# Graph attention on one core: two of five index windows unpacked later, and four filler matmuls fewer, at the seam between the sort and the block loop

## The chip, the cores and the metric

The kernel runs on one core of a Trainium2 chip. A core has five engines that run their own instruction streams in order and meet through semaphores: TensorE (PE, matmul), VectorE (DVE), ScalarE (ACT), GpSimd (POOL) and SyncE (SP, which here only issues DMA transfers). The metric is the device time of one execution in microseconds (us). Lower is better.

## The reference, cut to what matters

The problem is one graph attention layer: 4096 nodes with 64 features, 50000 edges, 4 heads, 64 output features for each head.

```python
x_proj[h] = x @ weight[h]
src_att = np.sum(x_proj[h, src_nodes] * att_src[h], axis=-1)
dst_att = np.sum(x_proj[h, dst_nodes] * att_dst[h], axis=-1)
s = src_att + dst_att
s = np.where(s > 0, s, 0.2 * s)
# for every edge i:
output[h, dst[i]] += np.exp(s[h, i]) * x_proj[h, src[i]]
# for every node:
output[h, dst] /= (sum of np.exp(s[h, i]) over its edges + 1e-8)
```

The result has 4096 rows of 256 numbers (4 heads by 64).

## The kernel before, in words

**Stages.** The first 109 us or so sort the edges, in two rounds of a sorting network on DVE, into 16 groups of 256 source nodes each and, inside a group, by destination. After that the destinations are taken in 33 blocks (`ND`) of 125 nodes (`BD`). A block has 16 stretches of edges, one for each source group, and each stretch is a row of 128 slots (`W2`). An edge slot is a pair of small numbers: its destination within the block and its source within the group.

**The windows.** The sorted keys lie in DRAM. Five indirect gathers (L362, issued by POOL) bring 128 rows of 128 keys each into `win`. Window `i` of the five holds the rows of eight blocks, 8`i` to 8`i`+7. `Windows.unpack(i)` (L439 to L447) takes one window apart. Two DVE operations (L441, L442) cut the key into its two parts, two more operations (L445, L446) turn these into bf16 and subtract the block's offset, and one transfer on the SP queue (L447) writes 64 KB into the DRAM table `bin_dram` (`gat_bins` in the profile). For window 0, L445 and L446 run on DVE. For the other four windows they run on POOL.

**One block.** `Blocks.load(b)` (L466) reads row `b` of the table, 8 KB, and repeats it over all 128 partitions, 1 MB in all, into one of four `bc` buffers. `onehot(b)` (L483) compares it with the partition number on DVE (L493 and L495), which gives 0/1 matrices `oh`. `gather(b, c)` (L499), for three chunks `c` of 6, 6 and 4 source groups, multiplies them on PE with the node table `xa` and the destination table `adb` (L514, L516, L520). ACT then takes the exponentials `ex` (L522) and a copy `xs` (L524) from PSUM. `weights(b)` (L534, DVE) forms the edge weight `wv`, and `values(b)` (L542, DVE) the products `val`. `sums(b, k)` (L560 and L567, PE) adds up the edges of each destination in the PSUM tile `acc`. The sink's `take` copies `acc` out on ACT (L621, L623), `project` multiplies with the weights on PE (L629), `invert` and `give` (L634, L642, DVE) divide, and the SP queue writes the 125 rows out (L644).

**The order of the work** is written out by hand, under a manual schedule, so each engine runs its instructions in the order of the code. Step `b` of `Blocks.run` is: load of block b+4, values(b), the first gather of block b+1, project(b-1), sums(b,-1), the other two gathers of block b+1, invert(b-1), onehot(b+2) with weights(b+1) between its two halves, give(b-1), sums(b,0), sums(b,1). Blocks 0 and 1 are handled by hand before that loop, since the table is not in DRAM yet: `spread` (L472) repeats their rows with matmuls on PE (L479) and copies (L481) instead of a transfer.

**The fillers.** `busy(n)` (L711) issues n matmuls of 128x512 (L715) whose result nobody reads. They go into a PSUM tile with the tag of `acc`, of which there is one. They stand at three places: 9 in the sort, 11 after `longest`, and 3 ahead of the block loop.

The seam that the change touches reads, shortened:

```python
        busy(11)
        win.unpack(0)
        ...
            blocks.spread(1, c, win.tb[:, 0], lambda t: NT + t, S.copy if c < 2 else V.tensor_copy)
        ...
        for i in range(1, NI):
            win.unpack(i)
        blocks.sums(0, 1)
        busy(3)
        blocks.onehot(2)
        blocks.weights(1)
        blocks.run(1)
```

Of the kernel before, what the change touches and what calls it, by code (L numbers as in the profile page):

```python
# [38 lines left out]
def kernel(ctx: ExitStack, tc: tile.TileContext, x: bass.AP, edge_index: bass.AP,  # L39
# [8 lines left out]
    NI = -(-ND // 8)  # L48
# [288 lines left out]
    def longest(pool, pp, *sides):  # L337

        ps = pp.tile([1, len(sides), P], F32, name="mx_ps")
        for i, (ws, we) in enumerate(sides):  # L340
            mx = pool.tile([P, ws.shape[1]], F32, name=f"mx{i}")
            V.tensor_tensor(out=mx[:], in0=we[:], in1=ws[:], op=OP.subtract)
            mx1 = pool.tile([P, 1], F32, name=f"mxr{i}")
            V.tensor_reduce(out=mx1[:], in_=mx[:], axis=AX, op=OP.max)
            T.transpose(out=ps[:, i, :], in_=mx1[:], identity=ident[:])
        V.tensor_reduce(out=most[:, 2 - len(sides):2], in_=ps[:], axis=AX, op=OP.max)
# [18 lines left out]
    def group(pool, pp, start, between=(), busy=None):  # L365

        raw = pool.tile([P, L], F32, name="raw")
        fetch(pool, skey1, start, W1, raw, 1)
        kr = pool.tile([P, L], F32, name="kr")
        S.activation(out=kr[:], in_=raw[:], func=ACTF.Identity, bias=goff[:, 0:1])  # L370
        sgn = below(pool, kr[:], L, nb2, ND, 8 * NI)
        so = Sorter(pool, raw)
        so.rows(9)
        st = Stretches(pool, counts(pool, pp, sgn, 8 * NI, [sel2[:]])[0])
        if between:
            busy(9)
        ki = pool.tile([P, L], I32, name="ki")
        quiet = lambda keys: None
        store(skey2, so.runs(ki, FINE, [lambda keys: st.count(), *(between or (quiet, quiet)),
                                        *(lambda keys, f=f: f() for f in st.steps(0))]))  # L380
        return st
# [72 lines left out]
    class Blocks:  # L454
# [124 lines left out]
            self.onehot(1)  # L579
            self.weights(0)  # L580

        def run(self, first=0):
            for b in range(first, ND):
                self.load(b + 4)
                self.values(b, 2 if b == ND - 1 else 1)
                self.gather(b + 1, 0)
                if b:
                    self.sink.project(b - 1)
                self.sums(b, -1)
                self.gather(b + 1, 1)  # L590
                self.gather(b + 1, 2)

                if b:
                    self.sink.invert(b - 1)
                self.onehot(b + 2, halves=(0,))
                self.weights(b + 1)
                self.onehot(b + 2, halves=(1,))
                if b:
                    self.sink.give(b - 1)
                self.sums(b, 0)  # L600
                self.sums(b, 1)
            self.sink.project(ND - 1)
            self.sink.invert(ND - 1)
            self.sink.give(ND - 1, 2)
# [61 lines left out]
    def advance(pool, ws, we, w, what):  # L666

        n = ws.shape[1]
        at = pool.tile([P, n], F32, name=f"at{what}")
        gone = pool.tile([P, n], F32, name=f"gone{what}")  # L670
        V.tensor_tensor(out=gone[:], in0=ws[:], in1=we[:], op=OP.is_ge)
        V.tensor_scalar(out=at[:], in0=ws[:], scalar1=-1.0, scalar2=float(P * L), op0=OP.mult, op1=OP.add)
        V.tensor_tensor(out=at[:], in0=at[:], in1=gone[:], op=OP.mult)
        V.tensor_tensor(out=at[:], in0=at[:], in1=ws[:], op=OP.add)
        V.tensor_scalar(out=ws[:], in0=ws[:], scalar1=float(w), scalar2=None, op0=OP.add)
        return at
# [24 lines left out]
    with ExitStack() as st:  # L701
        so2 = st.enter_context(tc.tile_pool(name="sort2", bufs=1))
        blocks = Blocks(st, Finish(st))

        class Lent:


            def tile(self, shape, dt, name):
                return blocks.sink.psf.tile(shape, dt, name=name, tag="pf")

        def busy(n):  # L711

            t = blocks.psa.tile([P, L], F32, name="warm", tag="acc")
            for i in range(n):
                T.matmul(out=t[:], lhsT=identb[:], rhs=adb[:, 0:4, 0:P], start=True, stop=True)  # L715


        kb0 = so2.tile([P, W2], I32)
        t0 = so2.tile([P, 2, W2], I32)
        tb0 = so2.tile([P, 2, W2], BF16)  # L720

        def relative(keys):
            V.tensor_scalar(out=kb0[:], in0=keys[:, 0:W2], scalar1=goff[:, 0:1], scalar2=None, op0=OP.add)

        def split(keys):
            V.tensor_scalar(out=t0[:, 0, :], in0=kb0[:], scalar1=8, scalar2=None, op0=OP.logical_shift_right)
            V.tensor_scalar(out=t0[:, 1, :], in0=kb0[:], scalar1=SG - 1, scalar2=None, op0=OP.bitwise_and)
            S.copy(out=tb0[:], in_=t0[:])
            for c in range(len(CH)):
                blocks.spread(0, c, tb0[:], lambda t: RUN * t, S.copy)  # L730

        stretches = group(so2, Lent(), wi1[:], (relative, split), busy)
        win = Windows(cst, stretches.to[0][:])
        for c in range(len(CH)):
            blocks.onehot(0, *CH[c])
            blocks.gather(0, c)
        stretches.rest()
        longest(so2, Lent(), (ws1, we1), (ws2, we2))
        V.tensor_scalar(out=over[:], in0=most[:, 0:1], scalar1=float(W1), scalar2=None, op0=OP.is_gt)
        V.scalar_tensor_tensor(out=over[:], in0=most[:, 1:2], scalar=float(W2), in1=over[:], op0=OP.is_gt, op1=OP.max)  # L740
        busy(11)
        win.unpack(0)
        for b in range(2, 5):
            blocks.load(b)
        blocks.weights(0)
        blocks.values(0)
        for c in range(len(CH)):
            blocks.spread(1, c, win.tb[:, 0], lambda t: NT + t, S.copy if c < 2 else V.tensor_copy)
            if c == 1:
                blocks.onehot(1, *CH[0])  # L750
        for c in (1, 2):
            blocks.onehot(1, *CH[c])
        blocks.sums(0, -1)
        blocks.gather(1, 0)
        blocks.sums(0, 0)
        blocks.gather(1, 1)
        blocks.gather(1, 2)
        for i in range(1, NI):
            win.unpack(i)
        blocks.sums(0, 1)  # L760
        busy(3)
        blocks.onehot(2)
        blocks.weights(1)
        blocks.run(1)
        again = nc.values_load(over[0:1, 0:1], min_val=0, max_val=1, skip_runtime_bounds_check_because="0 or 1")
    order.close()

# [1 line left out]
    with tc.If(again > 0):  # L769
        n1 = room(0, EL)  # L770
        with tc.tile_pool(name="all", bufs=1) as al:
            total = al.tile([P, ND, AW], F32)
            V.memset(total[:], 0.0)
            with tc.For_i(0, n1, W1):
# [5 lines left out]
                with tc.For_i(0, m2, W2):  # L780
                    with ExitStack() as st:
                        win = Windows(st.enter_context(tc.tile_pool(name="win", bufs=1)), advance(al, ws2, we2, W2, 2)[:])
                        for i in range(NI):
                            win.unpack(i)
                        blocks = Blocks(st, Total(total))
# [42 lines left out]
```

## Time and profile before

| quantity | value |
|---|---|
| median of 14 runs | 290.75 us (288.94 to 292.1) |
| the profiled execution's own time | 291.22 us |
| its span, first to last instruction | 289.4 us |
| mean granted TensorE clock | 0.869 of full speed |
| busy: DVE, PE, ACT, POOL | 259.2, 204.7, 190.9, 34.1 us |
| the block loop, L542 of block 1 to the last result | about 131.8 to 283 us |

The profile gives times in microseconds from the span's start. A row of its timeline has the start, the duration, the engine, the line of the kernel, what the operation writes and reads, and, in square brackets, how long the engine stood idle before it and what ended that idle time. "PEld" is PE's loading of stationary operands, "SPq" an issue on the SP queue. Shares of busy time are averages over stages with different limits, so they don't tell which engine sets the end in one stage.

### The profile page before, as it was taken

To read this page: it belongs to the slowest core of one execution; us is meant where nothing else is said; L and a number is where in the kernel's file an instruction comes from. 1 tells how busy PE (TensorE), PEld (TensorE's weight loads), DVE (VectorE), ACT (ScalarE), POOL (GpSimd) and SP (SyncE) were. 2 spreads that over 40 slices of the span, in tenths; PEclk is the share of its full clock that TensorE was granted. 3 is DMA by queue.
4 is the path that set the end of the run, shared out by engine and by line. 5 is a ranking of instruction groups with operands and counts; after the bars stand their busy time and mean duration, and the time that the engine had idled before them with its cause. 6 is when DMAs were issued, how large, how long until landed. Compare 5 with 4: busy or idle time off the path is not lost.

```text
span 289.4 us, 8530 instructions
## 1 busy us (share of the span) xinstructions
PE 204.7 (71%) x3531; PEld 194.6 (67%) x3531; DVE 259.2 (90%) x526; ACT 190.9 (66%) x392; POOL 34.1 (12%) x81
## 2 busy tenths in 40 slices
PE   0011899970000055769999999999999999999990
PEld 0010599960000025558999999999999999999980
DVE  5999999993599999858999999999999999999970
ACT  2960720022599938554888888888888888888860
POOL 7882000001100001851000000000000000000000
PEclk9999975555555559997999999999999999999997
DMA  3016000000100001495676776767686868675011
GB/s 111 0 46 119 0 2 0 0 2 36 36 0 0 0 0 40 143 348 186 202 280 229 275 240 254 263 233 273 226 285 220 292 206 297 215 284 186 23 38 43
DMA packets 12688, 40.77 MB, mean 141 GB/s; under 512 B 1840, under 2 KB 8272, under 8 KB 8672
## 3 DMA queue, kind: packets, MB, share of 16 engines
q1 hardware_dynamic: 10128, 37.91, 36.9%
q10 hardware_dynamic: 1808, 1.56, 2.3%
q0 software_dynamic: 704, 0.66, 1.2%
q8 instruction: 30, 0.49, 0.7%
q14 instruction: 18, 0.15, 0.2%
HBM read 35.08 MB, written 5.05 MB: 139 GB/s over the span
## 4 chain that ended last, share of the span: by engine, by line


## 5 line engine op out<-in xcount | busy, mean ns | idle before, releaser
L524 ACT CAST xs<-ps 128x1200 bf16<-128x1200 f32 (+1 forms) x99 | 104.1, 1052 | 0.0
L542 DVE TENSOR_TENSOR val<-xs,wv 128x4096 bf16<-128x4096 bf16 (+1 forms) x34 | 75.4, 2219 | 0.4 <-ACT xs L524 0.2
L516 PE MATMUL ps<-adb,oh 128*128 128x136 bf16 x528 | 62.1, 224 | 0.0
L514 PE MATMUL ps<-xa,oh 128*128 128x72 bf16 x528 | 59.4, 197 | 3.7 <-DVE oh L493 2.1
L567 PE MATMUL acc<-xs,val 128*128 128x125 bf16 x1024 | 61.8, 218 | 0.0
L567 PEld LDWEIGHTS <-val 128*128 128x128 bf16 x1056 | 58.5, 98 | 0.3 <-DVE val L542 0.3
L516 PEld LDWEIGHTS <-oh 128*128 128x128 bf16 x528 | 49.5, 99 | 1.5 <-issue 1.3
L514 PEld LDWEIGHTS <-oh 128*128 128x128 bf16 x528 | 47.3, 99 | 3.2 <-DVE oh L493 3.2
L281 PE MATMUL cnt_ps<-sgn,sel 128*128 128x17 f32 (+1 forms) x6 | 1.6, 387 | 60.4 <-ACT sgn L273 41.1
L493 DVE TENSOR_SCALAR oh<-bc,pF 128x4096 bf16<-128x4096 bf16 (+2 forms) x37 | 42.5, 1148 | 0.8 <-ACT bc L481 0.8
L281 PEld LDWEIGHTS cnt_ps<-sgn,sel 128*128 128x128 f32 x6 | 1.4, 320 | 60.4 <-issue 60.4
L522 ACT ACTIVATE ex<-ps 128x96 bf16<-128x96 f32 (+1 forms) x99 | 25.0, 252 | 25.8 <-PE ps L520 25.7
L202 DVE TENSOR_TENSOR sA<-sB 128x256 f32<-128x256 f32 (+2 forms) x104 | 37.2, 399 | 1.5
L202 DVE TENSOR_TENSOR sB<-sA 128x256 f32<-128x256 f32 (+2 forms) x98 | 35.1, 399 | 1.3
L520 PE MATMUL ps<-xa,oh 128*128 128x72 bf16 x528 | 33.6, 198 | 0.1
L520 PEld LDWEIGHTS <-oh 128*128 128x128 bf16 x528 | 26.5, 99 | 0.2 <-DVE oh L495 0.2
L420 PEld LDWEIGHTS at_ps<-uv,xT 64*128 64x128 f32 x130 | 25.7, 307 | 0.2 <-issue 0.2
L420 PE MATMUL at_ps<-uv,xT 64*128 64x4 f32 x130 | 25.8, 335 | 0.0
L495 DVE TENSOR_SCALAR oh<-bc,pF 128x2048 bf16<-128x2048 bf16 (+2 forms) x37 | 25.6, 692 | 0.0
L270 ACT ACTIVATE junk<-kr,nb 128x512 f32<-128x512 f32 x33 | 23.8, 722 | 1.1
L629 PE MATMUL pf<-Wbd,aT 128*128 128x128 f32 (+1 forms) x132 | 23.3, 299 | 0.5 <-ACT aT L621 0.5
L560 PEld LDWEIGHTS <-xs 128*128 128x128 bf16 x528 | 18.7, 97 | 0.4
(141 smaller groups left out, 230.5 us busy)
## 6 DMA issues: line engine op xcount, KB each, us to landing
bc<-gat_bins SPq DMA_DIRECT2D x31, 1024.0 KB, 5.2
out_dram<-res SPq DMA_DIRECT2D x32, 125.0 KB
eD<-in_edge_index_dram ACTq DMA_DIRECT2D x2, 195.0 KB, 3.5
eS<-in_edge_index_dram SPq DMA_DIRECT2D x2, 195.0 KB
gat_bins<-tb SPq DMA_DIRECT2D x5, 64.0 KB, 5.2
gat_sorted<-sA SPq DMA_DIRECT2D x1, 256.0 KB, 2.0
gat_sorted<-ki SPq DMA_DIRECT2D x1, 256.0 KB
win<-gat_sorted,to POOLq DMA_INDIRECT x5, 2.6
```

The costliest lines, as they stand in the source:

```text
L202: V.tensor_tensor(out=av(d[:], o, [2 * h, n], [1, h]), in0=av(s[:], 0, [2 * h, n], [1, h]), in1=av(s[:], h, [2 * h, n], [1, h]), op=op)
L270: S.activation(out=junk[:], in_=v, func=ACTF.Sign, bias=nbnd[:, b:b + 1], scale=1.0, accum_out=sgn[:, b:b + 1])
L420: T.matmul(out=ps[:, b, :], lhsT=xT[:, b * step:b * step + P], rhs=uv[:, k, :], start=(b == 0), stop=True, skip_group_check=True)
L493: V.tensor_scalar(out=oh[:, e], in0=bc[:, e], scalar1=pF[:, 0:1], scalar2=None, op0=OP.is_equal)
L495: V.tensor_scalar(out=av(oh[:], (2 * NT + t0) * W2, [W2, nt], [1, W2]), in0=av(bc[:], (2 * t0 + 1) * W2, [2 * W2, nt], [1, W2]), scalar1=p ...
L514: T.matmul(out=ps[:, i, P:P + XC], lhsT=hot(2 * t + 1), rhs=xa[:, 2 * t, :], start=(i % 2 == 0), stop=False, skip_group_check=True)
L516: T.matmul(out=ps[:, i, 0:S0], lhsT=hot(2 * t), rhs=adb[:, b, :], start=False, stop=False, skip_group_check=True)
L520: T.matmul(out=ps[:, i, P:P + XC], lhsT=hot(2 * NT + t), rhs=xa[:, 2 * t + 1, :], start=False, stop=True, skip_group_check=True)
L522: S.activation(out=av(ex[:], 2 * t0, [2, n], [2 * NT, 2 * H], [1, 2]), in_=av(ps[:], P, [PW, n], [1, 2 * H], [0, 2]), func=ACTF.Exp)
L524: S.copy(out=xs[:, t0:t0 + n, 0:P + XC], in_=ps[:, 0:n, 0:P + XC])
L542: V.tensor_tensor(out=av(val[:], h * Dout, [Dout, n], [C, NT], [1, Din]), in0=av(xs[:], S0, [0, n], [XW, NT], [1, Din]), in1=av(wv[:], h * ...
L567: T.matmul(out=self.to[k], lhsT=val[:, t, k * P:(k + 1) * P], rhs=xs[:, t, 0:self.n], start=apart and t == 0, stop=(t == NT - 1), skip_gro ...
```

## The change

Two edits. The 11 fillers after `longest` become 7. And of the four unpackings that stood in front of `sums(0, 1)`, those of windows 1 and 2 stay, while those of windows 3 and 4, which hold the rows of blocks 24 to 31 and 32, move into the block loop: `run` gets a dictionary of extra work, and runs window 3's unpacking at the end of step 1 and window 4's at the end of step 2. The three fillers ahead of the loop stay. Line numbers after these edits are one to two higher.

```diff
-        def run(self, first=0):
+        def run(self, first=0, also={}):
             for b in range(first, ND):
                 self.load(b + 4)
                 self.values(b, 2 if b == ND - 1 else 1)
...
                     self.sink.give(b - 1)
                 self.sums(b, 0)
                 self.sums(b, 1)
+                if b in also:
+                    also[b]()
...
-        busy(11)
+        busy(7)
         win.unpack(0)
...
-        for i in range(1, NI):
+        for i in range(1, 3):
             win.unpack(i)
         blocks.sums(0, 1)
         busy(3)
         blocks.onehot(2)
         blocks.weights(1)
-        blocks.run(1)
+
+        blocks.run(1, {i - 2: lambda i=i: win.unpack(i) for i in range(3, NI)})
```

More of the change, by code (lines that the diff above doesn't have):

```diff
@@ L757 @@
         blocks.gather(1, 2)
-        for i in range(1, NI):
+        for i in range(1, 3):
             win.unpack(i)
         blocks.sums(0, 1)
-        busy(3)
         blocks.onehot(2)
         blocks.weights(1)
-        blocks.run(1)
+        blocks.run(1, {i - 2: lambda i=i: win.unpack(i) for i in range(3, NI)})
         again = nc.values_load(over[0:1, 0:1], min_val=0, max_val=1, skip_runtime_bounds_check_because="0 or 1")
```

## The prediction

> **What bounds the kernel now.** I began with the slices of the page, to see where the engines are not full.
>
> ```profile
> PE   0011899970000055769999999999999999999990
> DVE  5999999993599999858999999999999999999970
> PEclk9999975555555559997999999999999999999997
> ```
>
> One slice is 7.2 us. The sort is DVE's and the block loop keeps PE and DVE both full. Between them (slices 16 to 18, about 116 to 137 us) both have dips, and the PE clock drops once. Next the busy times of that stretch, cut where the clock changes, and of the loop (columns: length, busy us of PE, PEld, DVE, ACT, POOL, then clock, DMA share, GB/s).
>
> ```profile
> 124.97:128.38 3.41, 2.12 (x39) 1.75 (x35) 0.89 (x6) 2.58 (x6) 2.79 (x6) 1.00 1.00 274
> 128.38:131.80 3.42, 1.25 (x21) 0.79 (x19) 2.60 (x6) 0.00 (x0) 2.29 (x2) 1.00 0.72 271
> 131.80:135.21 3.41, 3.41 (x51) 3.35 (x48) 3.41 (x3) 1.65 (x4) 0.00 (x0) 0.50 0.70 209
> 154.00:280.00 126.00, 125.54 (x2658) 125.06 (x2656) 123.81 (x162) 106.12 (x214) 0.00 (x0) 1.00 0.65 229
> ```
>
> PE was busy for 1.25 of 3.42 us, and in the next 3.41 us its clock was 0.50. In the loop it has full clock and no idle time to speak of. The timeline says why the gap is there:
>
> ```profile
> 125.25 0.22 DVE L442 TENSOR_SCALAR t<-win 128x128 int32<-128x128 int32 x1
> 126.83 0.32 DVE L441 TENSOR_SCALAR t<-win 128x128 int32<-128x128 int32 x1 [1.35 <-DMA win<-gat_sorted,to]
> 129.09 0.23 DVE L441 TENSOR_SCALAR t<-win 128x128 int32<-128x128 int32 x1 [1.89 <-DMA win<-gat_sorted,to]
> 129.37 1.38 DVE L493 TENSOR_SCALAR oh<-bc,pF 128x4096 bf16<-128x4096 bf16 x1
> ...
> 127.89 0.81 PE L715 MATMUL warm<-adb,identb 128*128 128x512 bf16 x3 [1.29 <-ACT aT L623]
> 130.81 0.21 PE L514 MATMUL ps<-xa,oh 128*128 128x72 bf16 x1 [2.11 <-DVE oh L493]
> ```
>
> DVE is in order. It waits 1.35 and 1.89 us for windows 3 and 4, whose data the loop needs only from block 24 on, and behind these waits stands block 2's one-hot, for which PE then waits 2.11 us. Those two waits are what the move takes away. Last, the filler and what follows it, and the queues that the moved work passes:
>
> ```profile
> 116.59 2.54 PE L715 MATMUL warm<-adb,identb 128*128 128x512 bf16 x11
> 118.96 1.47 PE L479 MATMUL ps<-tb,identb 128*128 128x256 bf16 x12
> 119.86 2.78 ACT L481 CAST bc<-ps 128x1536 bf16<-128x1536 f32 x2 [2.55 <-issue]
> 121.33 0.62 DVE L493 TENSOR_SCALAR oh<-bc,pF 128x1536 bf16<-128x1536 bf16 x1 [0.64 <-ACT bc L481]
> ...
> 118.51 3.00 POOL L362 DMA_INDIRECT win<-gat_sorted,to  x1 [0.30 <-issue]
> 129.65 2.02 POOL L446 TENSOR_SCALAR tb<-t,boff 128x128 bf16<-128x128 int32 x1
> ...
> 126.26 5.76 SPq L447 DMA_DIRECT2D gat_bins<-tb  x4
> 132.12 0.38 SPq L469 DMA_DIRECT2D bc<-gat_bins  x1
> ```
>
> **The change part by part.** It doesn't quite do what its few words say: windows 1 and 2 stay, and windows 3 and 4, of eight blocks each, move. These are the two with the waits, so for the time this is the part that counts.
>
> *Four fillers less.* Eleven start at 116.59 and the spread starts at 118.96, so one costs (118.96 - 116.59) / 11 = 0.215 us. Seven end at 118.10. The spread's operand is ready when window 0's L446 ends on DVE (117.89 + 0.36 = 118.25), so the spread starts at about 118.32, 0.64 us earlier. ACT's copy (119.86) and DVE's L493 (121.33, after a wait of 0.64 us for that copy) follow; DVE is free at 120.69, where values(0) ends, so it can use just those 0.64 us. From there to the end of sums(0,1), 126.60, DVE has no gap until 124.85 and PE and ACT follow it, so all of it shifts: -0.64 us. The bounds are 0 and -0.64; POOL decides (below). As a cost, the fillers kept PE busy. Afterwards the emptiest 3.4 us there have PE idle about 0.2 us before the spread and 0.9 us in it, some 68% busy; 62% (2.12 of 3.41) still kept the full clock above, 37% did not. So I charge nothing. If the clock fell, spread and gathers of about 3 us of PE work would cost up to 1.7 us.
>
> *Windows 3 and 4 leave the seam.* DVE finishes window 2 at 125.25 + 0.22, less 0.08 of overlap, so L493 of block 2 could start at 125.4 instead of 129.37, and with the 0.64 us at 124.8. It needs load(2): in the DMA packet records that load's last packet ends at 124.10, and from last packet to start, window 4 took 0.38 us (128.71 to 129.09), so 124.5, in time. The one-hot then ends at about 126.8 (1.38 and 0.86 us, as before), and weights(1) and values(1) at 129.5. What is late next is PE itself: the three fillers wait for `acc` to be copied (L623) and run from 127.89 to 128.70. Block 2's gather goes there instead of at 130.81: -2.11 us, and with the shift it starts at 128.06. Its third group (L520, first chunk) started at 131.59, 0.78 us behind L514. At full clock it took 0.55 us (122.69 to 123.24), another -0.23 us. Sum at this point: 131.59 to 128.61, -2.98 us.
>
> *The slow clock.* The first L520 of the next blocks start at 131.59, 137.71, 142.40 and 147.11: 6.12 us for the step with the half clock, then 4.69 and 4.71. After the change PE is never idle for more than 1.3 us at the seam (from the end of sums(0,1) to the three fillers), 62% of 3.4 us, the share that kept the clock. So the step should take 4.71: -1.41 us. Its bounds are 0 (the clock falls anyhow) and -1.41. [...]
>
> *The two unpackings in the loop.* On DVE, L441 and L442 take 0.27 us from start to next start (124.85 to 125.12), once in step 1 and once in step 2, ahead of values(2) and values(3). Is there room? In a step of the loop ACT's last ex ends at 150.64, DVE's L493 at 150.66, and L534 starts at 150.68, though DVE instructions without a wait start 0.08 us before the one in front has ended. So DVE has about 0.1 us of room in 4.71. PE's sums(4,0) start at 149.51, right behind values (149.39), so PE would wait: about 0.25 us in each step, and little is won back, since PE is full. +0.5 us; bounds 0.3 and 0.6.
>
> *POOL and DVE.* The moved L445 and L446 (0.29 and 0.60 us) run beside a DVE that is never idle. Where L445 and L446 of window 4 ran beside block 2's one-hot, L493 took 1.38 us against 1.26 later and L495 0.86 against 0.75: 0.12 and 0.11 us, 0.23 for an unpacking, and L446 stretched to 2.02 us. [...] By the rows it is -2.98 - 1.41 + 0.5 + 0.46 = -3.4. The same rows show L493 at 121.33 under way while POOL was still in its issue, so I stay near the rows: +0.4 for the unpackings and +0.2 for the issue.
>
> *The SP queue.* Two writes of 64 KB leave it ahead of load(5), which goes out before 132.12 and is used at about 141: no cost. In steps 1 and 2 they now stand between a result and the next load: out(0), write 3, load(6), and out(1), write 4, load(7). A write waits for POOL, and the load behind it too. POOL's L446 can wait for values(2) (2.28 us); about 3 us after DVE's L442 it is done, so load(6) goes out near 137 and lands 4.6 us later (132.12 to 136.69), 141.5. onehot(6), at 149.40 before, wants it near 145.5 to 146. The cover is 4 us. If POOL needs over 7 us, every us beyond that stops DVE, and load(7) does the same.
>
> **The sum.** -2.98 - 1.41 + 0.5 + 0.4 + 0.2 = -3.3 us. The profiled execution's 291.22 us (span 289.4) would be 287.9 and its span 286.1. It lies 0.47 us above the median of 290.75; against the median I take 287.5.
>
> **The rivals.** [...] (2) *Slower, through the SP queue.* POOL is shut out by DVE's unbroken stream, write 3 comes late, and load(6) and load(7) stand behind the writes. It decides from 7 us of delay on. At 9 us for each, the two loads cost 2 + 2 us and eat the -3.4 of the sum by the rows: +0.6, about even. At 11 us each it is 4 + 4 - 3.4 = +4.6, 295 us. For it: L446 at 2.02 us instead of 0.60. [...] (3) *No change*, if the 2.11 us come back as another wait at once, for load(3), say: its last packet ended at 128.46, 128.8 with the 0.38 us, and onehot(3) wants it at 129.5. A load late by 2.1 us or more would eat the gain of the wait. The margin is 0.7 us, and the DMA queue holds less ahead of it than before, so this is unlikely.
>
> **How the numbers follow.** The forecast has a chance of 0.73, rival 1 0.13, rival 2 0.08, no change 0.06. The forecast's own range is 286.4 to 288.5: both ends of the filler term, the clock term and the port term by the rows. The range for 8 in 10 goes on to 289.4 to take in rival 1. A difference under 0.3%, 0.87 us, is one that a measurement of this kernel can hardly tell from none. Faster by more than that: the forecast and most of rival 1, 0.84. Within it: 0.07. Slower: 0.09.
>
> **What would show it.** Right: no idle time of DVE before L441; block 2's L493 at about 125 us and its first gather matmul near 128; a clock of 1.00 from 108 us to the loop's end; the first L520 of block 5's gather at about 143.8 instead of 147.11, and 4.71 us a step after that. Wrong: a 0.50 in the clock between 118 and 135; a wait of L493 for `bc` in steps 3 to 6; L542 of steps 2 and 3 longer than 2.4 us, or L493 of block 1 held back to 121.5; SP's third and fourth write more than 5 us after their L442. If the first L520 of that gather comes no earlier than 146, the prediction is wrong whatever the reason.

## The result, and the profile after

The changed kernel took 286.76 us (median of 10 runs, 285.79 to 288.61) against 291.09 us before (median of 47 runs): ratio 0.9862, 95% interval 0.9839 to 0.9884, by the ratio some 4.0 us faster. On two other chips the same kernel gained half as much or less (e0 and e11 below). The profiled execution took 286.87 us with a span of 285.0, against 291.22 and 289.4. Ratios and intervals here and below leave out executions of e9, e11 and e12 that lie over 1.5% above their kernel's fastest; the medians include them, and the profile of e9 is of one of them.

One thing has to be put right first. The account of the change and the prediction above leave out an edit: **the changed kernel also drops the three fillers in front of the loop.** The diff shown above keeps that line; its true piece is

```diff
         for i in range(1, 3):
             win.unpack(i)
         blocks.sums(0, 1)
-        busy(3)
         blocks.onehot(2)
```

So seven fillers go, not four. The prediction costed a change that keeps three of them, and the runs below price that one too (e1).

After, the clock row of the page has no dip at the seam any more, and the three stretches that were shown of before (same limits and columns) are full:

```profile
PEclk9999975555555559999999999999999999999997
```
```profile
124.97:128.38 3.41, 3.19 (x66) 2.86 (x63) 3.31 (x5) 3.31 (x8) 3.41 (x4) 1.00 1.02 327
128.38:131.80 3.42, 3.42 (x73) 3.33 (x70) 3.42 (x6) 2.77 (x6) 2.66 (x1) 1.00 0.64 252
131.80:135.21 3.41, 3.38 (x75) 3.24 (x73) 3.41 (x6) 2.80 (x6) 2.99 (x2) 1.00 0.92 259
```

The timeline of the seam, the rows that answer to those of before (DVE behind window 2, the first matmul of block 2's gather, the fillers and what follows them):

```profile
124.82 0.22 DVE L442 TENSOR_SCALAR t<-win 128x128 int32<-128x128 int32 x1
124.96 1.31 DVE L493 TENSOR_SCALAR oh<-bc,pF 128x4096 bf16<-128x4096 bf16 x1
...
126.33 0.21 PE L514 MATMUL ps<-xa,oh 128*128 128x72 bf16 x1 [0.16 <-DVE oh L493]
...
116.72 1.67 PE L717 MATMUL warm<-adb,identb 128*128 128x512 bf16 x7
118.53 1.47 PE L479 MATMUL ps<-tb,identb 128*128 128x256 bf16 x12
119.43 2.78 ACT L481 CAST bc<-ps 128x1536 bf16<-128x1536 f32 x2 [1.99 <-issue]
120.90 0.62 DVE L493 TENSOR_SCALAR oh<-bc,pF 128x1536 bf16<-128x1536 bf16 x1
```

Block 2's one-hot follows window 2 at once, 4.41 us earlier than before (129.37), and its gather 4.48 us earlier (130.81), since no filler stands in front of it. But a new wait has come up in step 5. The POOL and SP rows show its origin:

```profile
132.22 2.42 POOL L445 CAST tb<-t 128x128 bf16<-128x128 int32 x1 [1.18 <-DVE t L441]
134.62 2.11 POOL L446 TENSOR_SCALAR tb<-t,boff 128x128 bf16<-128x128 int32 x1
137.12 2.42 POOL L445 CAST tb<-t 128x128 bf16<-128x128 int32 x1 [0.39 <-DVE t L441]
139.52 2.11 POOL L446 TENSOR_SCALAR tb<-t,boff 128x128 bf16<-128x128 int32 x1
...
136.76 0.32 SPq L447 DMA_DIRECT2D gat_bins<-tb  x1
137.13 0.42 SPq L469 DMA_DIRECT2D bc<-gat_bins  x1
...
141.65 0.32 SPq L447 DMA_DIRECT2D gat_bins<-tb  x1
142.02 0.43 SPq L469 DMA_DIRECT2D bc<-gat_bins  x1
142.54 0.29 SPq L646 DMA_DIRECT2D out_dram<-res  x1
142.88 0.32 SPq L469 DMA_DIRECT2D bc<-gat_bins  x1
...
149.78 1.29 DVE L493 TENSOR_SCALAR oh<-bc,pF 128x4096 bf16<-128x4096 bf16 x1 [0.96 <-DMA bc<-gat_bins]
```

POOL needs 4.5 us for an unpacking instead of 0.9. The write goes out when POOL is done (136.73, 141.63), and the load behind it one block step later than it would. load(7), out at 142.02, lands at 149.69, 7.7 us after its issue, and block 7's one-hot waits 0.96 us for it. (Of the sixteen landing events that the trace has for load(7), the eighth came 4.4 us after the issue.)

To tell the seam from the loop I use two spans of L542 starts in every run: the start of values(1), where the loop begins, and the time from values(1) to values(7). The nine or more steps behind that take 4.71 us each in every kernel but e5.

| kernel | values(1) starts | values(1) to values(7) | longest wait for `bc` |
|---|---|---|---|
| before | 131.77 | 29.48 | none |
| after | 127.29 | 29.54 | 0.96 |

The whole gain of this execution, 4.4 us of span, arose before values(1) (4.48 us). Inside the first steps the slow clock's loss (1.2 us over six steps of 4.71) was replaced by the two unpackings and the new wait (1.3 us).

### The profile page after: what moved, and what is told of

It is laid out like the page before. It is cut to its first block, busy times and chain, and to the rows that moved or that the text cites. A ratio compares the mean times of both kernels' runs of the same rounds, so it can differ in the third digit from the quotient of the medians.

```text
span 285.0 us, 8517 instructions
## 1 busy us (share of the span) xinstructions
PE 202.7 (71%) x3524; PEld 192.7 (68%) x3524; DVE 258.7 (91%) x526; ACT 190.9 (67%) x392; POOL 44.4 (16%) x81
## 4 chain that ended last, share of the span: by engine, by line
## 5 line engine op out<-in xcount | busy, mean ns | idle before, releaser
L542 DVE TENSOR_TENSOR val<-xs,wv 128x4096 bf16<-128x4096 bf16 (+1 forms) x34 | 75.4, 2219 | 0.4 <-ACT xs L524 0.2
L516 PE MATMUL ps<-adb,oh 128*128 128x136 bf16 x528 | 61.3, 223 | 0.0
L514 PE MATMUL ps<-xa,oh 128*128 128x72 bf16 x528 | 58.7, 196 | 2.1 <-ACT bc L481 1.1
L514 PEld LDWEIGHTS <-oh 128*128 128x128 bf16 x528 | 46.9, 98 | 1.4 <-DVE oh L493 1.4
L493 DVE TENSOR_SCALAR oh<-bc,pF 128x4096 bf16<-128x4096 bf16 (+2 forms) x37 | 42.5, 1148 | 1.2 <-DMA bc<-gat_bins 1.0
L520 PE MATMUL ps<-xa,oh 128*128 128x72 bf16 x528 | 33.3, 197 | 0.1
L520 PEld LDWEIGHTS <-oh 128*128 128x128 bf16 x528 | 26.2, 99 | 0.4 <-DVE oh L495 0.4
L420 PEld LDWEIGHTS at_ps<-uv,xT 64*128 64x128 f32 x130 | 25.7, 307 | 0.2 <-issue 0.2
L420 PE MATMUL at_ps<-uv,xT 64*128 64x4 f32 x130 | 25.8, 335 | 0.0
L495 DVE TENSOR_SCALAR oh<-bc,pF 128x2048 bf16<-128x2048 bf16 (+2 forms) x37 | 25.7, 694 | 0.0
```

Of the source, the lines that this page charges most:

```text
L420: T.matmul(out=ps[:, b, :], lhsT=xT[:, b * step:b * step + P], rhs=uv[:, k, :], start=(b == 0), stop=True, skip_group_check=True)
L493: V.tensor_scalar(out=oh[:, e], in0=bc[:, e], scalar1=pF[:, 0:1], scalar2=None, op0=OP.is_equal)
L495: V.tensor_scalar(out=av(oh[:], (2 * NT + t0) * W2, [W2, nt], [1, W2]), in0=av(bc[:], (2 * t0 + 1) * W2, [2 * W2, nt], [1, W2]), scalar1=p ...
L514: T.matmul(out=ps[:, i, P:P + XC], lhsT=hot(2 * t + 1), rhs=xa[:, 2 * t, :], start=(i % 2 == 0), stop=False, skip_group_check=True)
L516: T.matmul(out=ps[:, i, 0:S0], lhsT=hot(2 * t), rhs=adb[:, b, :], start=False, stop=False, skip_group_check=True)
L520: T.matmul(out=ps[:, i, P:P + XC], lhsT=hot(2 * NT + t), rhs=xa[:, 2 * t + 1, :], start=False, stop=True, skip_group_check=True)
```

## The experiments

Theory A was: the two DVE waits are the gain; the fillers matter only as far as they stand in front of something or hold the clock; the loads come late because they stand behind a write on the SP queue. The rivals are named in each expectation. Kernels of one set ran on one chip beside the kernel before.

**e3, the fillers alone.** The kernel before, with this edit:

```diff
-        busy(11)
+        busy(7)
-        busy(3)
```

> The kernel before with only the fillers cut: 7 after longest, none ahead of the loop; all four windows unpacked in the seam. Theory A: no gain, since DVE still waits for windows 3 and 4 until 126.8 and 129.1, whatever comes before, and the gather of block 2 starts at 130.8 as before; PE idles longer, so the slow clock comes as before or earlier: 0 to +1 us, ratio 1.000 to 1.003. Theory B (fewer fillers are the gain): 2 us or more faster, ratio under 0.993.

Measured: 291.43 against 291.55 us, ratio 0.9997 (0.9977 to 1.0018): no gain.

```profile
128.91 0.23 DVE L441 TENSOR_SCALAR t<-win 128x128 int32<-128x128 int32 x1 [2.98 <-DMA win<-gat_sorted,to]
...
130.63 0.24 PE L514 MATMUL ps<-xa,oh 128*128 128x72 bf16 x1 [3.90 <-DVE oh L493]
```
```profile
127.12:130.53 3.41, 0.00 (x0) 1.00 0.95 366
130.53:133.95 3.42, 3.32 (x44) 0.50 0.62 183
```

DVE is held by window 4 until 128.91 whatever stands ahead, PE waits 3.90 us instead of 2.11, and the clock falls (busy PE, then clock, in the second fence). Rival B is out.

**e2, the move alone.** The kernel before with the move, 11 and 3 fillers as they were. 

> The kernel before with only the move of windows 3 and 4 into steps 1 and 2; 11 and 3 fillers as before. Theory A: the move takes both DVE waits (3.2 us) and the slow clock away, but block 2's gather stands behind the three fillers at 128.7; first L520 near 129.2, steps of 4.7 to 4.9 us after it; 2.0 to 2.5 us faster than before (ratio 0.992), 0.5 us slower than with 7 fillers. Theory B (the fillers make most of the gain, the move little): within 0.3% of before.

Measured: 288.87 us, ratio 0.9907 (0.9884 to 0.993), -2.7 us. The first L520 of block 2's gather was at 129.03 (forecast 129.2), since the three fillers ran from 127.84; the clock stayed at 1.00. The move alone makes most of the gain.

**e1, the change as the prediction costed it.** The changed kernel with this edit:

```diff
         blocks.sums(0, 1)
+        busy(3)
         blocks.onehot(2)
```

> The changed kernel with the three fillers ahead of the loop put back: windows 3 and 4 moved, 7 fillers after longest, 3 ahead of the loop. This is the change that the prediction costed. Theory A (the three fillers hold block 2's gather back, since they wait for acc to be copied): first L520 of block 2's gather near 128.7 instead of 127.1, some 1.6 us slower than the changed kernel, so 2.6 to 2.9 us faster than before (ratio about 0.991), and the 0.96 us wait for load(7) stays or shrinks a little. Theory B (the three fillers are hidden as they were before): equal to the changed kernel, ratio 0.986.

Measured: 287.94 us, ratio 0.9867 (0.9843 to 0.9892), -3.9 us, more than theory A gave. The trace shows what A said of PE (fillers at 127.90, first L520 at 129.10, DVE idle 1.25 us before L534), but values(6) follows values(5) by 4.82 us, with a wait of 0.11 us for load(7). So A's mechanism is there and the time is nearer to B's. What the three fillers' removal won for block 2's gather in the changed kernel (1.5 us and more), the loop gave back in good part by running into the late load. By their ratios e1 and the changed kernel can't be told apart; they did not run side by side. Against e2, which has the four fillers after `longest` in addition, e1 is 0.9 us faster by the medians, though the intervals overlap a little (0.9843 to 0.9892 and 0.9884 to 0.993). In the profiles the way from DVE's last L344, just ahead of the fillers, to values(1) is 10.85 us in e1 and 11.45 in e2, 0.60 us less.

**e4, the writes of windows 3 and 4 on POOL's queue.** The changed kernel with

```diff
-            nc.sync.dma_start(out=bin_dram[...], in_=tb)
+            (G if i >= 3 else nc.sync).dma_start(out=bin_dram[...], in_=tb)
```

> The changed kernel with the table writes of windows 3 and 4 issued on the POOL queue instead of SP's, so that no load of a block stands behind them. Theory A (load(7) comes late because it stands behind write 4, which waits for POOL): load(6) goes out near 132.4 and load(7) near 137.3, no wait of L493 for bc, 0.9 to 1.0 us faster than the changed kernel, ratio to before about 0.983. Theory B (load(7) is late because the DMA engines are crowded after the seam, whatever the order): the wait of about 1 us stays, equal to the changed kernel.

Measured: 287.23 us, ratio 0.9844 (0.9815 to 0.9872). Its SP queue:

```profile
133.32 0.33 SPq L646 DMA_DIRECT2D out_dram<-res  x1
133.71 0.33 SPq L469 DMA_DIRECT2D bc<-gat_bins  x1
138.21 0.29 SPq L646 DMA_DIRECT2D out_dram<-res  x1
138.54 0.32 SPq L469 DMA_DIRECT2D bc<-gat_bins  x1
```

Each load follows the result at once and no wait for `bc` is left, as A has it, although load(7) took 7.2 us to land here too. In this execution the clock had come up only at 117.65, so its seam was later (values(1) at 128.55), and 0.53 us of PE idle time in step 3 ended in "issue". The 0.9 to 1.0 us that A gave does not show in the times: the interval overlaps that of the changed kernel (0.9839 to 0.9884).

**e0, the changed kernel again**, on another chip, beside e5, e6 and e7.

> The changed kernel once more, on the same chip as the three variants beside it, as their reference point: ratio 0.986 to before. Theory A (a load late behind write 4): again a wait of about 1 us of L493 for bc in step 5. Theory B (chance): the wait is absent or elsewhere.

Measured: 289.58 us (287.05 to 291.32), ratio 0.993 (0.9894 to 0.9965). The wait for load(7) was there again, 1.04 us. But the gain was half as large, and the trace shows where the rest went (busy PE, then clock):

```profile
116.96:120.37 3.41, 2.25 (x11) 1.00 0.18 48
120.37:123.79 3.42, 1.29 (x13) 1.00 0.57 161
123.79:127.20 3.41, 3.41 (x46) 0.50 1.01 420
```
```profile
118.65 0.41 DVE L346 TENSOR_REDUCE most<-mx_ps 1x2 int32<-1x256 f32 x1 [1.47 <-PE mx_ps L345]
...
122.27 2.78 ACT L481 CAST bc<-ps 128x1536 bf16<-128x1536 f32 x2 [2.75 <-issue]
```

Twice a consumer of PE's results came late: DVE's L346 waited 1.47 us (0.36 in the profile after), and ACT's copy started 2.10 us after the spread (120.17) instead of 0.90. That left PE busy for 1.29 of 3.42 us, the clock fell to 0.50, and values(1) started at 130.82, 3.5 us later than in the profile after. So the clock can fall in the changed seam too, which the prediction charged at nothing. But most of the 3.5 us are the late results themselves: 1.1 us at L346 and 1.2 at the copy. Another 0.6 arose earlier (the clock came up at 113.55 instead of 107.95), and only 0.7 behind the copy, where the clock was slow.

**e5, the same unpackings later.**

```diff
-        blocks.run(1, {i - 2: lambda i=i: win.unpack(i) for i in range(3, NI)})
+        blocks.run(1, {6 * i - 12: lambda i=i: win.unpack(i) for i in range(3, NI)})
```

> The changed kernel with windows 3 and 4 unpacked at the ends of steps 6 and 12 instead of 1 and 2. Theory A (a write that waits for POOL holds its load back by some 4.7 us, and the next load then follows within 1 us and shares the DMA engines with it): each of the two late loads has such a follower, so two waits of about 1 us instead of one; 0 to 1 us slower than the changed kernel. Theory B (the DMA engines are crowded only in the first steps after the seam): no wait, about 1 us faster than the changed kernel.

Measured: 289.27 us, ratio 0.9929 (0.9892 to 0.9965), equal to e0. No wait for `bc` anywhere, though write 3 (162.20) and load(11) (162.57) went out a step late and load(12) followed at 163.43: load(11) landed 6.2 us after its issue, in time. So theory A's account of the follower is wrong. Other profiles say the same: in e2 load(7) had load(8) 0.86 us behind it and landed after 5.7 us, in e7 (below) the next load came 4.06 us later and load(7) took 7.7 all the same. That B's gain of 1 us does not show in the median fits other losses of the profile: two steps of 4.98 us for the unpackings, and five waits of L534 for ACT of 0.20 to 0.86 us, the longest behind 0.66 us of PE idle time that ended in "issue".

**e7, L445 and L446 of the moved windows on ACT.**

```diff
+            if i >= 3:
+                S.copy(out=tb[:, 1, :], in_=t[:, 1, :])
+                S.activation(out=tb[:, 0, :], in_=t[:, 0, :], func=ACTF.Identity, bias=boff[:, i:i + 1])
+            else:
```

> The changed kernel with the two bf16 operations (L445 and L446) of windows 3 and 4 on ACT instead of POOL. [...] Theory B (the wait comes from crowded DMA engines, or ACT is as tight as DVE): equal or slower.

Measured: 289.7 us, ratio 0.9948 (0.992 to 0.9976): no faster than e0 in the median. Locally the load is on time: ACT's two operations (0.30 and 0.40 us) end 0.75 us behind the result's issue, write 3 goes out at 134.97 with load(6) at 135.35, no wait for `bc`, and values(1) to values(7) takes 28.89 us against 29.77 in e0. The clock fell here too. The profiled execution was 2.2 us faster than e0's (288.4 against 290.56), the median was not: a gain of this size is lost in a spread of 3 to 4 us between executions.

**e6, only the writes.** The DVE and POOL operations of windows 3 and 4 are left out, the writes stay.

> The changed kernel with the unpacking of windows 3 and 4 left out: only their two table writes remain in steps 1 and 2, with the rows of windows 1 and 2 in their place. Theory A: DVE's 2 x 0.27 us are gone (0.5 us) and the writes wait for nothing, so the load wait (0.96 us) is gone too: 1.5 us faster than the changed kernel, ratio 0.981. If the operations on DVE cost nothing: 1.0 us faster. If the wait comes from the DMA engines: 0.5 us faster.

Measured: 288.42 us, ratio 0.9911 (0.9877 to 0.9944). values(1) to values(7) took 28.38 us: six steps of 4.71 and 0.1, with no wait for `bc`. This is the floor. Its seam was that of e0 (values(1) at 130.83; the clock fell here too), so the two can be compared: e0 without its wait takes 29.77 - 1.04 = 28.73, and DVE's four small operations cost 0.35 us. By e10 (below, 28.83, no wait) it is 0.45.

**e9, e10, e11, e12, a third chip:** 11 fillers in the changed kernel; the same with the writes on POOL; the changed kernel once more; no filler after `longest` at all.

> The changed kernel with 11 fillers after longest as before (none ahead of the loop, windows 3 and 4 moved). Theory A (in some executions the seam's emptiest 3.41 us now has PE busy for less than half, and the clock falls for the next 3.41 us; four fillers more keep it up): spread 0.4 to 0.6 us later, but no 0.50 in the clock between 115 and 135; equal to the changed kernel in its good executions or 0.4 us slower, 1 us faster in the median where the changed kernel's clock falls; narrower spread of the times. Theory B (the four fillers only delay the spread): 0.4 us slower than the changed kernel throughout.

> As e9_eleven, and the table writes of windows 3 and 4 on the POOL queue. Theory A (the load wait is a matter of the SP queue's order, and costs about 1 us): no wait of L493 for bc, 0.5 to 1 us faster than e9_eleven, the fastest of the four, ratio 0.982 to 0.985. Theory B (what the write no longer holds back comes back as another wait): equal to e9_eleven.

> The changed kernel as a reference point for the three variants on this chip: ratio 0.986 if the clock holds in the seam, 0.993 in sessions in which it falls in most executions.

> The changed kernel without any filler after longest. The spread starts no earlier than with 7, since it waits for window 0's numbers at about 118.3 anyhow. Theory A (fillers are there for the clock): some 3.41 us of the seam have PE busy for well under half whatever the phase, so the clock falls to 0.50 once between 118 and 130 in nearly every execution: 1.0 to 1.7 us slower than the changed kernel with its clock up. Theory B (the loss needs a far emptier stretch): equal to the changed kernel.

| kernel | median us, all runs | ratio to before, interval | values(1) | values(1) to values(7) | wait for `bc` |
|---|---|---|---|---|---|
| e9, 11 fillers | 290.39 | 0.9959 (0.9926 to 0.9991) | 131.97 | 29.91 | 1.18 |
| e10, 11 and POOL writes | 289.71 | 0.9938 (0.9911 to 0.9965) | 131.83 | 28.83 | none |
| e11, changed kernel | 290.54 | 0.9949 (0.9918 to 0.9981) | 130.92 | 29.61 | 0.88 |
| e12, no fillers | 288.21 | 0.9887 (0.9852 to 0.9921) | 129.43 | 29.31 | 0.73 |

e9 refutes its theory A: four fillers more neither kept the clock up nor narrowed the times (287.37 to 292.74). e10's trace shows why they can't: they run before the stretch that is empty.

```profile
119.19:122.60 3.41, 1.41 (x13) 1.00 0.62 175
122.60:126.01 3.41, 2.33 (x32) 0.50 1.16 389
126.01:129.43 3.42, 3.42 (x43) 0.50 0.86 314
```

In e10, too, ACT's copy came 3.06 us after the spread's start (119.13 to 122.19). The writes on POOL's queue took the load wait away and shortened the first steps by 0.78 us against e11 and 1.08 against e9; the times don't show it, since the intervals overlap, and e10 was not the fastest of the four as its theory A had it. e12's clock fell, as A said, but earlier and cheaper:

```profile
116.52:119.93 3.41, 0.69 (x7) 1.00 0.23 58
119.93:123.34 3.41, 2.99 (x14) 0.50 0.42 113
123.34:126.76 3.42, 3.20 (x72) 1.00 1.00 410
```

The slow 3.4 us fall on the spread, which is short, and the gathers have full clock again; in e11 they fall on the gathers (0.50 from 123.93 to 127.34). Theory A had e12 1.0 to 1.7 us slower than the changed kernel with its clock up. By the ratios it is 0.7 us slower than that (0.9862, on another chip), and 1.8 us faster than e11 beside it. The intervals of e12 and e11 overlap by a little, so I call this likely, not shown. No fillers and POOL writes together, the version that these runs point to, was not tried.

**The seam, part by part.** The columns are L346's wait for PE, the time from the spread's start to ACT's copy, the time from that copy to values(1), and when the clock was 0.50.

| profile | L346 waits | spread to copy | copy to values(1) | clock at 0.50 |
|---|---|---|---|---|
| after | 0.36 | 0.90 | 7.86 | not in the seam |
| e5 | 0.39 | 1.45 | 7.85 | not in the seam |
| e0 | 1.47 | 2.10 | 8.55 | 123.79 to 127.20 |
| e11 | 1.60 | 2.16 | 8.59 | 123.93 to 127.34 |
| e7 | 0.41 | 1.43 | 9.14 | 122.91 to 126.33 |
| e10 | 0.43 | 3.06 | 9.64 | 122.60 to 129.43 |
| e12 | 1.59 | 1.51 | 7.86 | 119.93 to 123.34 |

A stretch at half clock behind the copy cost 0.7 to 1.3 us, two in a row 1.8. In every row with a fall a late result stands ahead of it, and in the rows from e5 down the late results cost 0.6 to 2.5 us.

## Why the prediction came out right, and where it did not

The direction, the place and the size hold: -3.3 us forecast; -4.0 us measured for the kernel as it is, and -3.9 us for e1, the kernel that the sum described. That the total is so near is in part luck: the terms missed in both directions. By its steps:

1. **The two DVE waits were the bound of the seam.** Right: e2 has most of the gain, e3 none. Block 2's one-hot was forecast for 124.8 and came at 124.96; values(1) was to end at 129.5 and ended at 129.59.
2. **"PE itself is late next", behind the three fillers.** Right for the kernel costed (e1: first L520 at 129.10, forecast 128.6), wrong for the changed kernel, which has no such fillers: 127.11. This is the edit that the prediction left out. It made the gather 1.5 us earlier than forecast; the first L520 of block 5's gather was at 141.77, not 143.8. A smaller misreading in this term: the 0.78 us from L514 to L520 were put down to the clock, but the clock fell only at 131.80, and what L520 (131.59) waited for was the end of DVE's L495 (130.68 + 0.86). The changed kernel has the same 0.78 us at full clock (126.33 to 127.11); e1 has 0.55.
3. **The fillers after `longest`, -0.64.** Right: -0.43 at DVE's L493 (121.33 to 120.90), with this profile's seam 0.13 us later to begin with, and -0.60 in e1 against e2. On the third chip e9 and e11, which differ by the same four fillers, show no difference (0.9959 and 0.9949).
4. **The slow clock, -1.41.** Right in the first profile: at the spread PE was busy for 2.36 of 3.42 us, 69% (forecast 68%), and the clock stayed at 1.00. Wrong as a certainty: "I charge nothing" for the emptier seam failed on two other chips (e0, e11), where the gain was 2.0 and 1.5 us (ratios 0.993 and 0.9949) and the clock fell in the profile. The larger part of what was lost there is a cost that the prediction had no term for: results of PE that reach ACT and DVE late.
5. **The two unpackings on DVE, +0.5.** Right: 0.35 us (e0 against e6) to 0.45 (e10 against e6).
6. **POOL beside DVE, +0.4 and +0.2.** Too dear. No run shows the 0.2 us for POOL's issue: block 1's L493 started at 120.90, while POOL was in its issue until 121.64. For the unpackings DVE lost next to nothing:

```profile
132.22 2.28 DVE L542 TENSOR_TENSOR val<-xs,wv 128x4096 bf16<-128x4096 bf16 x1
134.51 1.25 DVE L493 TENSOR_SCALAR oh<-bc,pF 128x4096 bf16<-128x4096 bf16 x1
```

   These are the durations of a step without POOL beside it (2.28 and 1.26). Both had started with POOL's operation or ahead of it (132.22 and 132.22, 134.51 and 134.62). L495 started at 135.82, inside POOL's L446 (134.62 to 136.73), and took 0.77 us instead of 0.75; in the next step it took 0.78. It was POOL that was stretched: L445 took 2.42 us instead of 0.29, values(2) and 0.14 us more, and L446 2.11 instead of 0.60.
7. **The SP queue, "no cost, the cover is 4 us".** This term was mis-sized: +0.96 us instead of 0, and a wait of L493 for `bc` was one of the prediction's own signs of being wrong. That load(6) went out near 137 as forecast (137.13) is luck: the write came 4.7 us behind DVE's L442 (132.08) and not 3, and the seam was that much earlier; in e1, the kernel costed, it went out at 138.97. And a landing was put at 4.6 us, from load(5) alone, while the page of before has a median of 5.2 us and single loads of that profile took up to 7.9. A load that goes out a step late has 6.7 us until its one-hot. In the seven profiles in which load(7) was so late it took 5.7 us (e2), 6.8 (e1), 7.4 (e12), 7.6 (e11), 7.7 (after and e0) and 7.9 (e9), and the waits are 0, 0.11, 0.73, 0.88, 0.96 and 1.04, and 1.18 us: what each landing has above 6.7. Where it went out in time (e4, e10) or its write waited for ACT alone (e7), landings of 6.6 to 7.7 us cost nothing. It is rival 2 in the small, its mechanism right, its point of decision (7 us of delay) too late: it began at 4.7. Why a landing takes 5.7 us or 7.9 is open.

Several slips cancelled in part. The fillers left out of the count brought 1.5 us more in the seam and the two terms for POOL beside DVE were 0.6 us too dear; the load wait took 0.96 us back: -3.3 - 1.5 - 0.6 + 0.96 = -4.4 us, the difference of the two spans.

**What stays open.** Why PE's results reached ACT and DVE late (by 0.5 to 2.5 us at one place or both) in the profiles of e0, e4 to e7 and e9 to e12, and not in those of before, after, e1, e2 and e3. The matmul records show no gap that explains it: the spread's first twelve took 1.47 us in e0 as in the profile after. The kernel before can hide such a delay, since its one-hot waits for window 4 in any case: e3's seam began 0.8 us later than that of before (L346 at 117.57 and 116.79), and its values(1) came no later (131.59 and 131.77). That would make the gain smaller wherever the results are late; it is likely and not shown, since no profile of before has late results.

## What to carry to other kernels

An in-order engine that waits for data needed twenty steps later is the first thing to move, and moving it can be worth more than the wait that PE shows (2.11 us here, 2.7 for the move alone): here a stretch with PE busy for 1.25 of 3.42 us was also followed by 3.41 us at a clock of 0.50. Before moving a step that issues a transfer, follow its queue: here write 4 went out 4.7 us behind DVE's L442, load(7) stood behind it, and block 7's one-hot waited 0.96 us. Before calling a late load covered, look at the spread of landings in the profile and not at one of them (4.9 to 7.9 us in the loop of before). Fillers should be judged by the stretch that they are to fill; those that run just before it bought nothing that these runs show (0.9959 with eleven, 0.9949 with seven).

## What the hardware showed that I had not expected

The two sides of the clock's fall lie close together. Around the seam I divided each of the fourteen profiles into nine stretches of 3.41 us, with a border wherever the clock changes, and in each stretch the clock was 1.00 or 0.50 throughout. Of the stretches at 1.00, the emptiest that was followed by 1.00 had PE busy for 1.70 us (e5, first fence), and the fullest that was followed by 0.50 had 1.68 us (e7, second fence; both by the profile's modelled ends):

```profile
108.46:111.87 3.41, 1.70 (x13) 1.00 0.00 0
111.87:115.29 3.42, 2.41 (x40) 1.00 0.23 84
```
```profile
119.50:122.91 3.41, 1.68 (x27) 1.00 0.56 176
122.91:126.33 3.42, 3.36 (x38) 0.50 1.04 400
```

Of the stretches at 0.50, one with PE busy for 2.86 us was followed by 0.50 (e4), one with 2.97 us by 1.00 (e11). These are single executions, and busy time alone does not account for the clock. In the sort, PE is busy without a break from 39.64 to 60.12 us in the profile before, with small f32 matmuls (L420, 64x4), and the clock stays at 0.50; it had fallen behind a stretch with PE busy for 3.35 of 3.42 us (the seventh and eighth of the slices that open the prediction have a 9 for PE and a 5 for the clock). And POOL's L445 stretched from 0.29 to 2.42 us beside a DVE without gaps, while DVE's L542 took 2.28 us as in a step without POOL.
